# Splitting fp32 weights for TensorE: from ScalarE and VectorE to two GpSimd DMAs and a ScalarE negation

## Chip, cores and metric

The kernel runs on one core of a Trainium2 chip. The metric is device time in microseconds (us) of one execution; lower is better. Engines are called PE (TensorE, matmul; PEld its weight loads), DVE (VectorE), ACT (ScalarE), POOL (GpSimd) and SP (SyncE, which issues the DMAs of the kernel before).

## The reference

Two transformer blocks run one after the other on 512 tokens of width 1024, all in fp32:

```python
# block 1
mod = silu(c) @ w_mod + b_mod                       # six vectors: shifts, scales, gates
h = rmsnorm(x, g_pre_mix) * (1 + sc1) + sh1         # the same for 256 context tokens
u, q, k, v = split(h @ w_in)
mix = concat([pool_mixer(u), neighbourhood_attention(q, k, v, k_ctx, v_ctx, rpb)]) @ w_out
x = x + gt1 * rmsnorm(mix)
y = square(relu(modulate(x) @ w_mlp_in)) @ w_mlp_out         # 1024 -> 4096 -> 1024
x = x + gt2 * rmsnorm(y)
# block 2
parts = rmsnorm(x) @ w_in_2                         # latent attention, a gated recurrence, memory attention
x = x + concat([rmsnorm(mla), hgrn, rmsnorm(mem)]) @ w_out_2
x = x + (silu(h2 @ w_gate) * (h2 @ w_up)) @ w_down           # 1024 -> 2816 -> 1024
```

## The kernel before

A product in fp32 precision is made of three fast matmuls. Each fp32 number is split into a half `hi`, rounded to the type fp32r, and a rest `lo = raw - hi`, also fp32r. Then `w x` is summed as `w_hi x_hi + w_hi x_lo + w_lo x_hi`, which is what `mm3` does with 512 tokens as the moving operand. Activations are split where they arise. Weights arrive from HBM as 128x1024 fp32 tiles (512 KB, eight 128x128 blocks), and each is split by `weights` (L590):

- `load_raw` (L584) has SP load the tile into one of 4 slots of the class `raw`.
- `copy` makes `hi`: a cast, on ACT or POOL.
- `tt` makes `lo`: a subtraction of `hi` from the raw tile, on DVE or POOL.
- `hi` and `lo` go into slots of the class `w`, of which there are 10, so five weights are held split at a time.

With one such weight PE does 8 blocks x 3 = 24 matmuls of 128x512 (`dense_tile`, `moving_k`); `chunked` asks for the weights of one output tile. Some weights are narrower: in the last stage a 128x1024 tile of `w_down` alternates with one of 128x256.

The order of the program is not written out by hand. Every instruction is recorded by `Plan.record` with its reads and writes, and `Plan.schedule` picks, with a table of costs (`Cost`, `Machine`), the order in which each engine gets them. That order is then fixed: every engine, and SP, takes its own instructions strictly in that sequence and waits at each for the semaphores that it needs. Slots are handed out in the plan, too, so a load waits until the last reader of its slot's former tile is done.

The stages, by time in the profile: the norm of x with the modulation vectors and `w_in_v` (to 68 us); projections, neighbourhood attention, pool mixer, `w_out`, memory keys and the first `w_mlp_in` tiles (to 291 us); the first feed-forward, `w_mlp_in` and `w_mlp_out` (to 651 us); a norm (to 672 us); `w_in_2`, `w_hi` and the start of the recurrence (to 780 us); recurrence, latent and memory attention, `w_out_2` (to 965 us); the second feed-forward, `w_gate`, `w_up`, `w_down` (to the end). The two feed-forward stretches are called dense below, the others mixed.

Everything that the plan issues is called in `Plan.issue`, so the profile gives nearly all instructions one line, L508; tiles are told apart by the names of their classes (`t`, `w`, `raw`, `bank`, `tmp`, `fixed`, `big`) or of the DRAM tensor. `bank` is a PSUM bank.

Of the kernel before, what the change touches and what calls it, by code (L numbers as in the profile page):

```python
# [9 lines left out]
F = mybir.dt.float32  # L10
R = mybir.dt.float32r
I32 = mybir.dt.int32
U8 = mybir.dt.uint8
AF = mybir.ActivationFunctionType
ALU = mybir.AluOpType
# [52 lines left out]
class Tag:  # L68
    def __init__(self, cls, shape, dtype, cap=None):
        self.cls, self.shape, self.dtype, self.cap = cls, shape, dtype, cap  # L70
        self.needs = [] if cls == "fixed" else [cls] + ([cap[0]] if cap else [])
        self.users = 0
        self.writer = [None, None]
        self.readers = [[], []]
        self.slot = None
        self.real = None
        self.owner = None


class View:  # L80
# [7 lines left out]
    def rows(self, i):  # L88
        v = self[64 * i:64 * i + 64]
        v.parts = (i,)  # L90
        return v

    def rearrange(self, pattern, **kw):
# [82 lines left out]
def inputs(args, kw):  # L176
    rest = list(args[0 if "out" in kw else 1:]) + [z for k, z in kw.items() if k not in ("out", "accum_out")]
    return [z for z in rest if isinstance(z, View)]


class Cost:
# [3 lines left out]
    def __init__(self, eng, fn, args, kw):  # L185
        self.eng, self.extra, self.tail, self.port = eng, 0, TAIL[eng], False
        self.strips, self.used = (0, 1, 2, 3), 0
        if eng == "PE":
            self.extra = 160
            self.pe(fn, args, kw)  # L190
        elif eng == "SP":
            self.time = 470
        else:
            self.other(fn, args, kw)

# [42 lines left out]
class Machine:  # L238
# [38 lines left out]
    def commit(self, c, op, t):  # L277
        if c.eng == "PE":
            fin = self.pe_end(t, c.time)
            for i in c.strips:  # L280
                self.strip[i] = fin
            self.issue, self.width = t + 14, len(c.strips)
            i = int(fin // TICK)
            self.ticks[i] = self.ticks.get(i, 0) + c.used
            return fin + c.extra
        fin = self.end(c, op, t)
        self.free[c.eng] = fin - c.tail
        if c.eng == "SP":
            self.dma = max(self.dma, t + 1150) + op.nbytes / 360.0
            return self.dma + 950  # L290
        if self.load(op):
            self.table = op.table[0]
        if c.port:
            self.port[c.eng], self.turn = fin, t
        return fin + c.extra
# [13 lines left out]
class Plan:  # L309
# [13 lines left out]
    def record(self, choices):  # L323
        op = Op()
        op.idx = len(self.ops)
        op.prio = op.idx + self.shift
        op.choices = []
        for eng, fn, args, kw in choices:
            op.choices.append((eng, fn, args, kw, Cost(eng, fn, args, kw)))
        eng, fn, args, kw = choices[0]  # L330
        out = kw.get("out", args[0] if args else None)
        outs = [z for z in (out, kw.get("accum_out")) if isinstance(z, View)]
        ins = [z for z in inputs(args, kw) if not any(z is o for o in outs)]
        op.writes = {id(z.tag): z.tag for z in outs}
        op.reads = {id(z.tag): z.tag for z in ins}
        op.nbytes = 4 * math.prod(out.shape) if eng == "SP" else 0
        op.table = None
        if fn == "activation":
            op.table = TABLES.get(kw.get("func", args[2] if len(args) > 2 else None))
        deps = set(self.fence)  # L340
        for z in ins:
            deps.update(w for w in (z.tag.writer[q] for q in z.parts) if w is not None)
        raw = set(deps)
        for z in inputs(args, kw):
            raw.update(z.tag.writer[q] for q in z.parts)
        for z in outs:
            for q in z.parts:
                if z.tag.writer[q] is not None:
                    deps.add(z.tag.writer[q])
                deps.update(z.tag.readers[q])  # L350
        for z in outs:
            for q in z.parts:
                z.tag.writer[q], z.tag.readers[q] = op.idx, []
        for z in ins:
            for q in z.parts:
                if z.tag.writer[q] != op.idx:
                    z.tag.readers[q].append(op.idx)
        op.allocs = []
        for t in list(op.writes.values()) + list(op.reads.values()):
            if t.owner is None:  # L360
                t.owner = op.idx
                op.allocs.append(t)
        for t in {**op.reads, **op.writes}.values():
            t.users += 1
        deps.discard(op.idx)
        op.need = len(deps)
        op.succ = []
        op.ready = [0.0] * len(op.choices)
        for d in deps:
            self.ops[d].succ.append((op.idx, d in raw))  # L370
        self.ops.append(op)
        return op
# [108 lines left out]
    def place(self, tag):  # L481
        if tag.real is None:
# [6 lines left out]
            else:  # L489
                tag.real = self.slots.tile([128, WIDTH[tag.cls]], tag.dtype, tag=f"{tag.cls}{tag.slot}", name=n)  # L490
                if tag.shape[1] != WIDTH[tag.cls]:
                    tag.real = tag.real[:, :tag.shape[1]]
# [24 lines left out]
U_AFTER = ((2,), (1,), (0,), ())  # L517
CTX_LOAD, CTX_NORM = 0, 3
CTX_AT = {4: (0, 1), 5: (2, 3), 6: (4, 5), 7: (6, 7)}
WIDTH = {"t": 528, "raw": 1024, "w": 1024, "big": 1664, "tmp": 16}  # L520
CAPS = {'t': 54, 'raw': 4, 'w': 10, 'big': 2, 'tmp': 32, 'bank': 8}


def later(name):
    def wrap(method):
        def call(self, *args, **kw):
            keep = self.plan.shift
            self.plan.shift = keep + LATER[name]
            try:
                return method(self, *args, **kw)  # L530
            finally:
                self.plan.shift = keep
        return call
    return wrap


class Builder:
    def __init__(self, tc, a):
        self.tc, self.a = tc, a
        self.nc = self.plan = Plan(CAPS)  # L540

# [46 lines left out]

    @later("weights")
    def weights(self, src, n, raw=None, engines=None):  # L590
        if raw is None:
            raw = self.load_raw(src, n)
        hi = self.plan.tile("w", [128, 1024], R)
        lo = self.plan.tile("w", [128, 1024], R)
        self.copy(hi[:, :n], raw[:, :n], engines or ("ACT", "POOL"))
        self.tt(ALU.subtract, lo[:, :n], raw[:, :n], hi[:, :n].bitcast(F), engines)
        return hi, lo
# [113 lines left out]
    def halves(self, x, n_tok):  # L711
        hi, lo = self.pair(n_tok)
        self.split(x[:, :n_tok], hi, lo)
        return hi, lo
# [1049 lines left out]
```

## Time and profile before

| | |
|---|---|
| median of 3 runs | 1384.15 us (1383.81 to 1390.59) |
| the profiled execution | 1385.12 us, its span 1383.3 us |
| PE busy | 1338.9 us, 97% of the span |
| DVE, ACT, POOL busy | 846.7 us (61%), 571.9 us (41%), 38.6 us (3%) |
| DMA | 148.47 MB, mean 107 GB/s |
| mean granted PE clock | 0.99 of full speed |

The span is the time between the first and the last instruction of the profiled execution; 1.8 us lie around it. Matmuls overlap, and the end of each is modelled, so a busy PE need not be a PE at its peak rate: how many matmuls a stretch of time holds says more. The time that an engine stood idle is put down to what ended the wait. The chain is followed back from the last instruction to whatever released it, step by step.

### The profile page before, as it was taken

How to read it: one execution, taken by the hardware profiler on the slowest of the kernel's cores; microseconds unless marked ns; L12 is line 12 of the kernel's file. 1: busy time of each engine (PE TensorE's matmuls, PEld its weight loads, DVE VectorE, ACT ScalarE, POOL GpSimd, SP SyncE). 2: the span in 40 equal slices, each digit the busy share in tenths (PEclk: the TensorE clock that was granted, in tenths of full speed). 3: DMA queues.
4: the chain of work that ended last, by engine and by line, in shares of the span. 5: the costliest groups of instructions: out<-in, count | busy, mean ns of one | idle time of the engine just before them, and what ended most of it. 6: DMA issues, size and time to landing. Idle time of an engine off the chain costs nothing.

```text
span 1383.3 us, 18475 instructions
## 1 busy us (share of the span) xinstructions
PE 1338.9 (97%) x7202; PEld 1068.7 (77%) x7202; DVE 846.7 (61%) x1544; ACT 571.9 (41%) x952; POOL 38.6 (3%) x58
## 2 busy tenths in 40 slices
PE   6999999999999999999899899999999999999999
PEld 4777777867887888887688677778788888888887
DVE  5787889784453743445845879998864443344432
ACT  4444466544242332334435656667433222232220
POOL 1021120000000000000000000000000000000000
PEclk9999999999999999999899999999999999999999
DMA  9654654232542233323233020211322223332231
GB/s 343 216 138 140 207 186 136 93 105 87 183 151 76 82 102 99 100 92 92 91 91 107 17 66 25 76 46 47 122 76 101 97 69 91 115 107 91 69 101 59
DMA packets 48663, 148.47 MB, mean 107 GB/s; under 512 B 5568, under 2 KB 7232, under 8 KB 48576
## 3 DMA queue, kind: packets, MB, share of 16 engines
q1 hardware_dynamic: 48576, 147.30, 33.4%
q8 instruction: 56, 0.92, 0.3%
q14 instruction: 31, 0.25, 0.1%
HBM read 143.61 MB, written 2.10 MB: 105 GB/s over the span
## 4 chain that ended last, share of the span: by engine, by line
PE 88%; DVE 8%; DMA 2%; issue 1%; ACT 1%; SPq 0%; DVEq 0%; ACTq 0%
PE bank L508 88%; DVE t L508 5%; ACT t L508 1%; DVE tmp L508 1%; DMA raw<-w_mod_b 1%; DVE fixed L508 1%; DVE bank L508 1%; DMA t<-w_mod_a 0%; SPq L508 0%; DMA raw<-w_in_qk 0%; DVE w L508 0%; DVE big L508 0%; ACT w L508 0%; ACT tmp L508 0%; DVEq L508 0%
## 5 line engine op out<-in xcount | busy, mean ns | idle before, releaser
L508 PE MATMUL bank<-t,w 128*128 128x512 f32 (+1 forms) x4716 | 1098.6, 391 | 9.3 <-DVE w L508 4.0
L508 PEld LDWEIGHTS bank<-t,w 128*128 128x128 f32 x4716 | 867.8, 189 | 212.5 <-DVE t L508 6.7
L508 DVE TENSOR_TENSOR w<-raw,w 128x1024 fp32r<-128x1024 f32 (+2 forms) x217 | 250.3, 1158 | 391.4 <-PE bank L508 250.2
L508 ACT CAST w<-raw 128x1024 fp32r<-128x1024 f32 (+2 forms) x214 | 212.0, 994 | 420.2 <-PE bank L508 383.2
L508 DVE TENSOR_TENSOR t<-t,t 128x512 f32<-128x512 f32 (+4 forms) x286 | 167.9, 610 | 35.0 <-ACT t L508 28.0
L508 ACT ACTIVATE t<-t 128x256 f32<-128x256 f32 (+2 forms) x192 | 100.9, 543 | 47.7 <-DVE t L508 32.9
L508 PE MATMUL bank<-t,t 128*64 128x128 f32 (+5 forms) x796 | 92.8, 281 | 6.9 <-DVE t L508 4.3
L508 PEld LDWEIGHTS bank<-t,t 128*128 128x128 f32 (+2 forms) x796 | 73.9, 161 | 23.6 <-DVE t L508 7.7
L508 PE MATMUL bank<-w,t 128*128 128x512 f32 x312 | 76.1, 396 | 0.0
L508 ACT COPY t<-bank 128x512 f32<-128x512 f32 (+3 forms) x93 | 47.9, 518 | 67.7 <-PE bank L508 64.4
L508 ACT ACTIVATE t<-bank 128x512 f32<-128x512 f32 (+2 forms) x74 | 43.4, 587 | 72.6 <-PE bank L508 71.6
L508 PEld LDWEIGHTS bank<-w,t 128*128 128x128 f32 x312 | 57.8, 188 | 15.1 <-ACT t L508 1.3
L508 ACT CAST t<-t 128x512 fp32r<-128x512 f32 (+2 forms) x77 | 44.2, 584 | 55.1 <-DVE t L508 53.5
L508 DVE TENSOR_TENSOR t<-bank,t 128x512 f32<-128x512 f32 (+3 forms) x86 | 56.8, 661 | 8.6 <-PE bank L508 5.4
L508 PE MATMUL bank<-t,fixed 128*32 128x256 f32 (+3 forms) x246 | 38.5, 498 | 13.3 <-DMA t<-w_mod_a 12.3
L508 DVE SCALAR_TENSOR_TENSOR t<-raw,fixed,t 128x512 f32<-128x512 f32 x56 | 43.0, 810 | 12.3 <-DMA raw<-w_mod_b 12.2
L508 PE MATMUL bank<-fixed,t 128*128 128x128 f32 (+2 forms) x292 | 46.8, 279 | 3.4 <-ACT t L508 1.5
L508 PEld LDWEIGHTS bank<-fixed,t 128*128 128x128 f32 x292 | 35.3, 161 | 15.1 <-issue 5.2
L508 DVE TENSOR_TENSOR t<-t 128x512 f32<-128x512 f32 (+1 forms) x68 | 37.9, 557 | 4.5 <-DMA t<-xP 4.1
L508 DVE SCALAR_TENSOR_TENSOR t<-t,fixed,t 128x512 f32<-128x512 f32 (+3 forms) x60 | 38.4, 676 | 1.2 <-ACT t L508 0.9
L508 ACT ACTIVATE t<-bank,fixed 128x512 f32<-128x512 f32 (+2 forms) x32 | 21.8, 682 | 33.2 <-PE bank L508 33.0
L508 PEld LDWEIGHTS bank<-t,fixed 128*32 128x32 f32 (+1 forms) x246 | 13.6, 131 | 27.2 <-ACT fixed L508 12.3
(93 smaller groups left out, 552.8 us busy)
## 6 DMA issues: line engine op xcount, KB each, us to landing
raw<-w_mod_b SPq DMA_DIRECT2D x32, 512.0 KB, 3.9
raw<-w_mlp_in SPq DMA_DIRECT2D x32, 512.0 KB, 3.6
raw<-w_mlp_out SPq DMA_DIRECT2D x32, 512.0 KB, 3.8
raw<-w_in SPq DMA_DIRECT2D x22, 512.0 KB, 3.6
raw<-w_gate SPq DMA_DIRECT2D x22, 512.0 KB, 3.2
raw<-w_up SPq DMA_DIRECT2D x22, 512.0 KB, 3.2
t<-w_mod_a SPq DMA_DIRECT2D x32, 256.0 KB, 6.0
raw<-w_out SPq DMA_DIRECT2D x16, 512.0 KB, 3.8
```

The source lines that it names most:

```text
L508: getattr(engines[eng], fn)(*[real(z) for z in args], **{k: real(z) for k, z in kw.items()})
```

## The change

For every weight that isn't already loaded, `weights` now takes one slot of 128x2048, half of it `hi`, half `lo`, and issues two DMAs from POOL's queue with an ACT instruction between them:

1. a DMA from HBM into `hi` whose destination type is fp32r, so that the transfer does the cast;
2. `lo = -hi` on ACT (an activation with scale -1);
3. a DMA from HBM of the same weight onto `lo` that adds: `lo = -hi + raw`.

The raw tile in SBUF, the cast and the subtraction go. The four `w_in_v` tiles (five loads) keep the old way, since they come with a `raw`. The class `w` has 5 slots of 128x2048 instead of 10 of 128x1024, the same five weights; the 4 `raw` slots stay, now for `w_in_v`, `w_mod_b`, `rpb_b` and `pool_w`. The planner gets costs for a DMA on POOL, and since it plans anew, the whole order changes in places.

```diff
@@ View
+    def halves(self):
+        n = self.shape[1] // 2
+        v = [self[:, n * i:n * i + n] for i in range(2)]
+        for i in range(2):
+            v[i].parts = (i,)
+        return v
@@ Cost
         elif eng == "SP":
             self.time = 470
+        elif fn == "dma_start":
+            self.time, self.tail = 1000, 0
@@ Machine.commit
-        if c.eng == "SP":
-            self.dma = max(self.dma, t + 1150) + op.nbytes / 360.0
+        if op.nbytes:
+            self.dma = max(self.dma, t + (1150 if c.eng == "SP" else 1600)) + op.nbytes / 360.0
             return self.dma + 950
@@ Plan.record
-        op.nbytes = 4 * math.prod(out.shape) if eng == "SP" else 0
+        op.nbytes = 4 * math.prod(out.shape) * (2 if "accum_op" in kw else 1) if fn == "dma_start" else 0
@@
-WIDTH = {"t": 528, "raw": 1024, "w": 1024, "big": 1664, "tmp": 16}
-CAPS = {'t': 54, 'raw': 4, 'w': 10, 'big': 2, 'tmp': 32, 'bank': 8}
+WIDTH = {"t": 528, "raw": 1024, "w": 2048, "big": 1664, "tmp": 16}
+CAPS = {'t': 54, 'raw': 4, 'w': 5, 'big': 2, 'tmp': 32, 'bank': 8}
@@ Builder.weights
+        pair = self.plan.tile("w", [128, 2048], R)
+        hi, lo = pair.halves()
         if raw is None:
-            raw = self.load_raw(src, n)
-        hi = self.plan.tile("w", [128, 1024], R)
-        lo = self.plan.tile("w", [128, 1024], R)
+            self.nc.gpsimd.dma_start(hi[:, :n], src)
+            self.nc.scalar.activation(lo[:, :n], hi[:, :n].bitcast(F), AF.Copy, scale=-1.0)
+            self.nc.gpsimd.dma_start(lo[:, :n], src, accum_op=ALU.add)
+            return hi, lo
         self.copy(hi[:, :n], raw[:, :n], engines or ("ACT", "POOL"))
         self.tt(ALU.subtract, lo[:, :n], raw[:, :n], hi[:, :n].bitcast(F), engines)
         return hi, lo
```

Three places show how instructions move. In the names, the part after the last underscore only numbers the tile; on POOL the first DMA with a name is the cast into `hi`, the second the addition onto `lo`.

The start on POOL, before: after the memsets come the splits of the first two `w_in_v` loads.

```order
L508 MEMSET fixed_2_68 128x256
L508 MEMSET tmp_3_70 128x1
L508 MEMSET t_5_74 128x8
...
L508 TENSOR_SCALAR w_47_179<-raw_28_127 128x512
L508 TENSOR_TENSOR w_49_184<-raw_28_127,w_47_179 128x512
```

The same place, changed:

```order
L517 MEMSET fixed_2_68 128x256
L517 MEMSET tmp_3_70 128x1
L517 DMA w_5_74<-w_in_u 128x1024
L517 MEMSET t_8_80 128x8
...
L517 DMA w_5_74<-w_in_u 128x1024
...
L517 TENSOR_SCALAR w_51_189<-raw_27_124 128x512
L517 TENSOR_TENSOR w_51_189<-raw_27_124,w_51_189 128x512
```

Both DMAs of the first `w_in_u` weight now stand ahead of the `w_in_v` splits; before, SP loaded that tile behind all of `w_mod_a`, `masks` and `pool_w`.

POOL in the second feed-forward, changed (before, POOL has nothing there, SP one load and DVE one subtraction for each weight):

```order
L517 DMA w_2014_9487<-w_up 128x1024
L517 DMA w_2017_9514<-w_gate 128x1024
L517 DMA w_2014_9487<-w_up 128x1024
L517 DMA w_2017_9514<-w_gate 128x1024
L517 DMA w_2022_9555<-w_up 128x1024
L517 DMA w_2025_9582<-w_gate 128x1024
L517 DMA w_2022_9555<-w_up 128x1024
L517 DMA w_2025_9582<-w_gate 128x1024
```

Weights go in twos: two casts, then the two additions. With one queue in order, the third cast is behind the second addition.

The last stage, `w_down`, on DVE, before:

```order
L508 TENSOR_TENSOR w_2612_11605<-raw_2594_11490,w_2606_11564 128x1024
L508 TENSOR_TENSOR w_2616_11618<-raw_2599_11524,w_2610_11577 128x256
L508 TENSOR_TENSOR t_2619_11625<-fixed_125_409,bank_2607_11570 128x512
L508 TENSOR_TENSOR w_2620_11651<-raw_2605_11561,w_2614_11610 128x1024
L508 TENSOR_TENSOR w_2624_11664<-raw_2609_11574,w_2618_11623 128x256
L508 TENSOR_TENSOR t_2627_11671<-fixed_251_936,bank_2615_11616 128x512
```

and what carries the weights there now, on POOL:

```order
L517 DMA w_2196_11224<-w_down 128x256
L517 DMA w_2195_11194<-w_down 128x1024
L517 DMA w_2200_11240<-w_down 128x1024
L517 DMA w_2196_11224<-w_down 128x256
L517 DMA w_2201_11268<-w_down 128x256
L517 DMA w_2203_11280<-w_down 128x1024
L517 DMA w_2200_11240<-w_down 128x1024
L517 DMA w_2201_11268<-w_down 128x256
```

On DVE only the additions of the residual are left. On POOL the rows read: cast of w_2196, addition of w_2195, cast of w_2200, addition of w_2196, casts of w_2201 and w_2203, additions of w_2200 and w_2201: between the cast of a weight and its addition, which waits for ACT's negation, stand one or two DMAs of others.

## Rows read from the trace of the kernel before

**Rows 1.** The page: busy time of the engines, and the chain that ended last by engine.
```profile
PE 1338.9 (97%) x7202; PEld 1068.7 (77%) x7202; DVE 846.7 (61%) x1544; ACT 571.9 (41%) x952; POOL 38.6 (3%) x58
PE 88%; DVE 8%; DMA 2%; issue 1%; ACT 1%; SPq 0%; DVEq 0%; ACTq 0%
```
**Rows 2.** Stretches: from:to, length, busy us (xinstructions) by engine, PE clock, DMA share, GB/s.
```profile
0.00:68.00 68.00, 54.48 (x333) 40.97 (x334) 42.73 (x89) 30.69 (x58) 6.63 (x18) 1.00 0.80 282
68.00:291.00 223.00, 213.24 (x1289) 167.41 (x1287) 188.98 (x433) 117.26 (x225) 25.51 (x33) 1.00 0.45 140
291.00:651.00 360.00, 359.44 (x1577) 290.37 (x1577) 174.70 (x231) 123.25 (x163) 0.00 (x0) 1.00 0.36 112
651.00:672.00 21.00, 14.95 (x60) 10.22 (x58) 21.00 (x33) 11.87 (x19) 0.00 (x0) 0.93 0.03 10
672.00:780.00 108.00, 104.19 (x792) 83.72 (x794) 68.01 (x132) 53.15 (x90) 0.53 (x1) 0.94 0.31 93
780.00:965.00 185.00, 177.69 (x1357) 139.18 (x1346) 162.34 (x392) 117.64 (x252) 5.93 (x6) 0.97 0.17 52
965.00:1380.00 415.00, 414.80 (x1820) 336.83 (x1819) 188.52 (x238) 118.01 (x149) 0.00 (x0) 1.00 0.28 91
```
**Rows 3.** Waits of PE: what released it, us in total, times, longest.
```profile
PE bank L508 <- DMA t<-w_mod_a: 12.3, 1, 12.3
PE bank L508 <- DVE t L508: 9.6, 15, 1.6
PE bank L508 <- ACT t L508: 5.2, 10, 1.3
PE bank L508 <- DVE w L508: 4.0, 1, 4.0
```
**Rows 4.** The stretches of rows 2, instructions on `w` tiles alone (DVE third, ACT fourth).
```profile
0.00:68.00 68.00, 35.84 (x149) 27.38 (x150) 8.56 (x7) 7.22 (x7) 3.77 (x4) 1.00 0.80 282
68.00:291.00 223.00, 150.72 (x687) 114.40 (x685) 26.48 (x21) 26.14 (x25) 0.00 (x0) 1.00 0.45 140
291.00:651.00 360.00, 355.53 (x1539) 286.85 (x1539) 83.10 (x68) 68.88 (x66) 0.00 (x0) 1.00 0.36 112
651.00:672.00 21.00, 14.95 (x60) 10.22 (x58) 1.23 (x1) 2.08 (x2) 0.00 (x0) 0.93 0.03 10
672.00:780.00 108.00, 91.84 (x378) 72.97 (x378) 21.95 (x18) 18.26 (x18) 0.00 (x0) 0.94 0.31 93
780.00:965.00 185.00, 108.41 (x405) 77.27 (x405) 19.98 (x20) 14.98 (x18) 5.41 (x5) 0.97 0.17 52
965.00:1380.00 415.00, 414.46 (x1816) 336.39 (x1815) 88.99 (x82) 74.44 (x79) 0.00 (x0) 1.00 0.28 91
```
**Rows 5.** The chain that ended last, in order of time: start us, us, what.
```profile
5.49 6.67 DMA t<-w_mod_a
...
670.68 1.15 DVE w L508
```
**Rows 6.** DMA issues: count, KB each, median us from issue to landing.
```profile
raw<-w_mlp_in SPq DMA_DIRECT2D x32, 512.0 KB, 3.6
...
raw<-w_in_v SPq DMA_DIRECT2D x3, 512.0 KB, 6.0
...
raw<-w_down SPq DMA_DIRECT2D x8, 128.0 KB, 2.7
```
**Rows 7.** Instructions on `w` and `raw` tiles: ns min/median/max, first and last start, forms.
```profile
L508 DVE TENSOR_TENSOR w<-raw,w x217: 419/1225/1997, 25.7 to 1365.7; 128x1024 fp32r<-128x1024 f32 x88, 128x512 fp32r<-128x512 f32 x12, 128x256 fp32r<-128x256 f32 x8, 128x768 fp32r<-128x768 f32 x1
L508 ACT CAST w<-raw x214: 407/1050/1063, 24.6 to 1359.1; 128x1024 fp32r<-128x1024 f32 x102, 128x512 fp32r<-128x512 f32 x3, 128x768 fp32r<-128x768 f32 x2
L508 POOL TENSOR_TENSOR w<-raw,w x3: 1262/1272/1692, 16.3 to 898.3; 128x512 fp32r<-128x512 f32 x3
L508 DVE SCALAR_TENSOR_TENSOR t<-raw,fixed,t x56: 739/747/1559, 73.6 to 381.0; 128x512 f32<-128x512 f32 x56
L508 SPq DMA_DIRECT2D raw<-w_mod_b x32: 327/328/524, 62.2 to 374.5; - x32
```

## The prediction, made before the change was run

> **What bounds the kernel now.** I read the page first: PE is busy 97% of the span, and 88% of the chain that ended last is PE, 8% DVE [rows 1]. The table of stretches then separates two kinds of time [rows 2]. In the dense stretches, 291 to 651 and 965 to 1380 us, PE is idle for 0.6 and 0.2 us and starts 1577 and 1820 matmuls, one each 228 ns in both. Weights come early enough there, so a faster way to split them gains nothing; it can only lose. In the other stretches PE is idle for 68 - 54.5 = 13.5, then 9.8, 6.1, 3.8 and 7.3 us. Of the first, 12.3 us are one wait for the first `w_mod_a` tiles [rows 3], which no split shortens. That leaves 28.2 us, and it is all that a relief of DVE can give directly. The clock adds a little: it is granted at 0.93, 0.94 and 0.97 of full speed between 651 and 965 us [rows 2], the stretches in which PE also stood idle; that is 0.07 x 21 + 0.06 x 108 + 0.03 x 185 = 13.5 us of lost clock, part of which returns if the waits do.
>
> The waits of PE say what ends this idle time [rows 3]: DVE's work on activations 9.6 us in 15 short waits, ACT's 5.2 us, and one wait of 4.0 us for the subtraction of a weight. The chain shows that one: at 670.7 us it runs through a DVE instruction on `w`, just behind the norm in which DVE was busy for all 21 us [rows 5, 2].
>
> **What is removed.** 217 subtractions on DVE and 3 on POOL, all but the five of `w_in_v` [rows 7]. In the dense stretches that takes 83 and 89 us off DVE [rows 4] at no gain. In the mixed ones it takes 8.6 + 26.5 + 1.2 + 22.0 + 20.0 = 78 us [rows 4] from 43 + 189 + 21 + 68 + 162 = 483 us that DVE is busy there [rows 2], 16%. Of the 28.2 us, the wait for a subtraction goes whole: 4.0 us. For the other 24.2 the bounds are 16% of the 9.6 us that PE waits for DVE's activations, 1.5 us, and all of it. I take 6.5, near the lower end, since the DVE instructions that PE waits for depend on each other and keep their durations; what goes is a subtraction queued between them. **Gain 10.5 us, bounds 5.5 and 28.2.** Late next there: the same DVE work on activations.
>
> ACT's cast becomes a negation of the same 128x1024 elements, 1.05 us by the cast's row [rows 7]; I cost the difference at nothing. SP's loads of weights go, one issue of 0.33 us each [rows 7], off the path.
>
> **What is added on the DMA engines.** One transfer of 512 KB becomes two, one of which also reads its destination. At 112 GB/s the 16 engines are busy 36% of the time, at 91 GB/s 28% [rows 2], so full use is 311 to 325 GB/s and 512 KB take 1.6 to 1.7 us of all engines. No cast and no addition is in this trace. The bounds for both together are two plain transfers, 3.3 us, and four, if each costs double, 6.6 us. I take three, 5.0 us, because only the addition has a second source. PE uses a weight in 24 x 228 ns = 5.5 us, so 5.0 us stays hidden behind it, with the engines some 90% busy. The Trainium skill ("Collectives: The Full Stack", The bandwidth ceiling) says that an adding transfer reads two sources and so runs at half the rate of a copy, the add itself being free. By that, addition and cast are 3.3 + 1.65 us, what I take; no run so far shows it.
>
> **What is added on POOL.** 215 weights, two DMAs each. The nearest rows for the time that one holds POOL are 0.33 us for an SP issue and 1.27 us for a POOL instruction on half a tile [rows 7]. A landing takes 3.6 us where the DMA engines are little used, 6.0 us where they are 80% busy [rows 6, 2]. In the dense stretches the queue runs cast, cast, addition, addition. The second addition waits for the second cast's landing and ACT's 1.05 us, and the next cast is behind it. So two weights hold the queue for a landing, a negation and two issues: 3.6 + 1.05 + 0.7 = 5.3 us at least, 6.0 + 1.05 + 2.5 = 9.6 us at most. PE needs two in 10.9 us. Hidden at both ends; the cover is the five slots, and if a landing rose to 7.4 us it would be gone.
>
> The last stage has less cover. There a tile of 1024 columns alternates with one of 256, 24 + 6 matmuls, so two weights are wanted every 6.8 us. The same sum gives 5.3 to 9.6 us: a loss of 0 to 2.8 us for each of the eight pairs (the narrow tiles number 8 [rows 6]), 0 to 22 us. I take a landing of 4.5 us, nearer to the 3.6 us of this kind of load, and an issue in the middle, 0.8: 7.15 us, **2.5 us in all**.
>
> **What is moved.** The first `w_in_u` weight is now cast at the very start, beside the loads on SP whose last, at 5.5 us, gates PE until 12.2 us [rows 5]. In the first stretch 282 GB/s keep the engines 80% busy [rows 2]: full use is 353 GB/s, and 512 KB more cost 1.5 us, the cast and the addition at three transfers 4.5 us; nothing, if they fill gaps. I take **2.0 us**, since SP no longer loads that tile later in the stretch. ACT's negation of it waits for the landing, and behind it on ACT are the first splits of x, which wait for the same loads. POOL's additions stand ahead of the pool mixer's and the memsets; these had long waits before them and only hold POOL.
>
> **The sum.** The profiled execution took 1385.1 us: a span of 1383.3 and 1.8 around it. 1385.1 - 10.5 + 2.5 + 2.0 = 1379.1 us. The median of the three runs is 1.0 us lower than that execution, so I forecast **1378 us**, and on the same scale the own range of this case is 1370 to 1385 us.
>
> **Rivals.**
> *The DMA engines become the bound (slower).* If the cast, too, costs two transfers, a weight takes 6.6 us of all engines where PE uses it in 5.5. The point that decides is 5.5 us. The price is 1.1 us for each of the 68 + 82 = 150 weights of the dense stretches [rows 4], 170 us: about 1550 us. For it: the engines change the type of each word and nothing here shows at what rate. Against it: only one of the two reads two sources.
>
> *The chain cast, negation, addition is late (slower).* Landings of 6.0 us, which 90% busy engines may well give, cost the last stage 22 us instead of 2.5. In the mixed stretches ACT holds its queue 2.4 us longer at each of some 62 negations, 149 us of 331 us busy there [rows 2]; ACT is 1% of the chain [rows 1], 14 us, 4% of that work, so about 6 us reach the end. 1378 + 20 + 6 = 1404 us.
>
> *DVE and POOL hold each other off (slower).* Single DVE instructions took 1997 instead of 1225 ns and 1559 instead of 747 [rows 7]: some 0.8 us in which another engine's instruction had to end. If each of the 124 DMAs that POOL issues for those 62 weights did this to DVE or was held by it, that is 99 us; DVE is on the chain for 8% of 1383, 111 us, 23% of its work there, so 23 us arrive: 1401 us. Against it: most DVE instructions show their median. The Trainium skill ("SBUF — State Buffer", SBUF: two separate sides) warns of just this: a DMA issued from GpSimd has its descriptors written there, and a DVE copy in a two-port mode locks it out, so it advises the ACT or SP queue. What the trace shows fits a lock of some kind; it shows no such DMA.
>
> *The whole idle time goes (faster).* If DVE's queue was the cause of all short waits, 28.2 us and most of the 13.5 us of clock return: 1385 - 41 + 2 = 1346 us at best. Against it: ACT and the matmuls' own order end part of the waits [rows 3].
>
> **How the numbers follow.** About 0.5%, 6.9 us, is what a measurement can tell from no change. I give the forecast 0.44, nearly half of it below 1377.2 us; the large gain, below 1370 us, 0.18; the late chain and the lock together 0.22, between 1386 and 1440 us, 0.05 of it within the bound; the DMA bound 0.16. Faster: 0.21 + 0.18 = 0.39. Same: 0.23 + 0.05 = 0.28. Slower: 0.17 + 0.16 = 0.33. The range of 1355 to 1450 us leaves out nearly all of the DMA bound and the far end of the large gain, some 2 in 10. Both signs hold much of it, so I repeat the likeliest case's own range, 1370 to 1385.
>
> **What would show it.** Right: DVE some 250 us less busy, one matmul each 228 ns in both dense stretches, no wait of PE for a `w` tile, landings near 4 us. The DMA bound would show as PE waiting for additions all through 291 to 651 us with the DMA share near 1; the late chain as such waits in the last 55 us alone and as ACT waiting for casts; the lock as DMA issues far over 1.3 us on POOL or DVE instructions far over their medians. A wait of PE in a dense stretch makes the forecast wrong.

## The result, and the profile after

The changed kernel takes **1404.45 us** (median of 4 runs, 1399.54 to 1406.1) against 1384.76 us (1383.81 to 1390.59): a ratio of 1.0127, interval [1.009, 1.0165]. Slower, outside the likeliest case's own range and within the wide one. Its profiled execution took 1404.54 us.

The page after: busy time, the DMA queue of POOL, the chain by engine.

```profile
PE 1343.8 (96%) x7202; PEld 1074.4 (77%) x7202; DVE 620.4 (44%) x1339; ACT 571.2 (41%) x951; POOL 337.0 (24%) x479
...
q0 software_dynamic: 61920, 210.00, 66.3%
...
PE 76%; DVE 8%; DMA 4%; issue 4%; ACT 2%; POOL 1%; DVEq 0%; POOLq 0%; ACTq 0%
```

DVE lost 226 us of work [rows 1], yet PE's share of the chain fell from 88 to 76%: DMA and issue have come onto it. The stretches, moved along with the program's own stages (columns as in [rows 2]):

```profile
0.00:70.00 70.00, 54.64 (x306) 39.08 (x307) 39.47 (x83) 26.92 (x50) 11.78 (x25) 1.00 0.92 308
70.00:300.00 230.00, 217.07 (x1317) 173.17 (x1317) 159.79 (x409) 120.97 (x230) 55.56 (x76) 0.99 0.75 194
300.00:660.00 360.00, 357.72 (x1554) 288.45 (x1553) 101.13 (x166) 122.29 (x160) 91.35 (x128) 1.00 0.83 193
...
980.00:1400.00 420.00, 414.66 (x1816) 336.17 (x1814) 108.70 (x161) 116.40 (x149) 115.24 (x161) 1.00 0.80 184
```

The dense stretches hold nearly as many matmuls as before (1554 for 1577 and 1816 for 1820), with the DMA engines at 0.83 and 0.80 instead of 0.36 and 0.28 [rows 2]. Where the time is lost shows best when one follows the weight matmuls: there are 5028 with a weight tile in every kernel, and the table gives how much later than before some of them start (us, counted from 0, worked out from the instructions' start times in one profiled execution of each kernel; the rows below `after` are the experiments of the next section). The 450th ends the front (projections and the first attention heads), the 2250th the first feed-forward, the 3450th lies just behind the start of the second, the 4800th just ahead of its last stage.

```
kernel                        450th   2250th   3450th   4800th     last
before (starts at)            176.7    620.7   1021.5   1334.0   1379.8
after                         +15.3    +13.0    +15.2    +15.0    +19.1
ctl_all_old                    -0.6     -2.6     +2.8     +2.8     +2.9
e1_front_old                   -0.1     -3.3     -4.5     -4.9     -1.0
e4_front_new                  +10.9     +8.8    +15.0    +15.1    +15.3
e6_add64                       +8.0     +5.8     +0.9     +0.8     +0.8
e12_neg_pool                   +9.8     +7.9    +11.2    +11.0    +14.6
e21_mod_no_wait                +7.4     +4.0    +10.9    +10.7    +14.8
e22_before_no_wait             -2.3     -2.5     -4.8     -4.8     -4.8
e19_price_front                +1.8     +0.2     +7.9     +7.6    +11.7
e10_price                      +4.4     +5.3     -2.3     -1.8     +3.1
e16_price6000                  +2.9     +8.8    +18.0    +17.9    +21.5
e13_price_add64                +0.1     +3.0     -3.1     -3.6     -3.5
e14_price_front_old            -0.5     +1.3     +1.0     +2.1     +7.3
e17_price_both_old             -0.2     +1.0     -0.1     +0.8     +0.8
e3_both_old                    -1.3     -3.8     -7.2    +38.7    +38.9
e20_price_mid_new              -1.9     -1.4     -1.7     -1.6     -1.6
```

So the 19 us are +15 in the front, +4 in the last stage, and about nothing between. In the front, the stretches of the kernel before and of the one after, at the same places in the program:

```profile
24.00:68.00 44.00, 43.95 (x273) 34.41 (x266) 32.00 (x66) 20.87 (x37) 1.19 (x4) 1.00 0.74 260
68.00:115.00 47.00, 45.25 (x284) 37.24 (x283) 36.83 (x86) 20.63 (x41) 11.29 (x13) 1.00 0.56 160
115.00:177.00 62.00, 59.71 (x391) 46.15 (x390) 50.88 (x139) 31.66 (x63) 5.83 (x8) 1.00 0.53 166
```

```profile
27.00:75.00 48.00, 45.28 (x264) 34.29 (x265) 30.94 (x69) 16.80 (x29) 5.52 (x10) 1.00 0.90 293
75.00:127.00 52.00, 48.55 (x287) 39.10 (x287) 33.98 (x86) 23.88 (x45) 17.09 (x21) 0.97 0.88 226
127.00:192.00 65.00, 60.02 (x387) 47.48 (x386) 40.38 (x124) 33.88 (x65) 13.45 (x20) 0.97 0.59 154
```

The DMA engines are nearly full there until 127 us, where before they had a quarter to a half of their time free. Of the 15 us some 3.5 are clock (an estimate: 0.03 of 52 and of 65 us). It was granted at 0.50 of full speed, the lower of its two levels, from 76 to 79 and from 141 to 144 us, each time just behind waits of PE (1.3 and 0.5 us, then 4.4 us). What waits for the DMA engines, after, in the first 192 us (us in total, times, longest), and one of these waits on ACT:

```profile
DVE t L517 <- DMA raw<-w_mod_b: 22.7, 7, 6.4
...
ACT w L517 <- DMA w<-w_in_qk: 13.3, 5, 6.9
ACT w L517 <- DMA w<-w_in_u: 7.1, 1, 7.1
```

```profile
72.32 1.06 ACT L517 ACTIVATE w<-w 128x1024 fp32r<-128x1024 f32 x1 [7.14 <-DMA w<-w_in_u]
```

Before, DVE waited 4.5 us for `w_mod_b` up to 177 us, and ACT 12.5 us for the loads of `w_in_qk` and `w_in_u` that it cast. The `w_mod_b` loads are not weights of matmuls: DVE multiplies them into the modulation vectors that are wanted much later. But DVE takes its instructions in the plan's order, so a late load holds back the attention's work behind it. ACT is held in the same way, here 7.1 us by a negation whose cast had not landed. Both are on the chain that ended last (start us, us, what):

```profile
83.38 9.09 DMA w<-w_in_qk
92.49 1.06 ACT w L517
...
116.31 9.13 DMA raw<-w_mod_b
...
132.08 5.82 DMA raw<-w_mod_b
...
140.18 10.33 PE bank L517 x63
```

PE's own waits hardly name a weight at all:

```profile
PE bank L517 <- DMA t<-w_mod_a: 12.9, 2, 12.7
PE bank L517 <- DVE t L517: 11.4, 11, 4.4
PE bank L517 <- ACT t L517: 9.5, 13, 1.4
...
PE bank L517 <- DMA w<-w_down: 3.3, 3, 1.6
```

The last of them is the last stage, seen in the chain there (start us, us, what):

```profile
1354.13 8.41 DMA w<-w_down
...
1380.14 4.06 DMA w<-w_down
1384.30 1.07 ACT w L517
1385.66 6.34 DMA w<-w_down
```

Issues and landings (count, KB, median us to landing; then ns min/median/max that one DMA holds POOL, where a cast is near the minimum and an addition near the median):

```profile
w<-w_mlp_in POOLq DMA_DIRECT2D x64, 512.0 KB, 6.1
...
raw<-w_mod_b SPq DMA_DIRECT2D x32, 512.0 KB, 5.6
...
w<-w_down POOLq DMA_DIRECT2D x32, 512.0 KB, 5.5
w<-w_in_qk POOLq DMA_DIRECT2D x16, 512.0 KB, 6.5
```

```profile
L517 POOL DMA_DIRECT2D w<-w_mlp_in x64: 542/865/892, 266.2 to 596.1; - x64
```

### The profile page after: what moved, and what is told of

It reads as the page before. It is cut to its first block, busy times and chain, and to the rows that moved or that the text cites. A ratio compares the mean times of both kernels' runs of the same rounds, so it can differ in the third digit from the quotient of the medians.

```text
span 1402.8 us, 18605 instructions
## 1 busy us (share of the span) xinstructions
PE 1343.8 (96%) x7202; PEld 1074.4 (77%) x7202; DVE 620.4 (44%) x1339; ACT 571.2 (41%) x951; POOL 337.0 (24%) x479
## 4 chain that ended last, share of the span: by engine, by line
PE 76%; DVE 8%; DMA 4%; issue 4%; ACT 2%; POOL 1%; DVEq 0%; POOLq 0%; ACTq 0%
PE bank L517 76%; DVE t L517 6%; DMA w<-w_down 1%; ACT t L517 1%; DMA raw<-w_mod_b 1%; POOL w L517 1%; DVE tmp L517 1%; DMA w<-w_in_qk 1%; DMA w<-w_in 1%; DMA w<-w_mem_v 1%; DVE big L517 1%; DVE bank L517 0%; DMA w<-w_out 0%; ACT w L517 0%; DVE fixed L517 0%
## 5 line engine op out<-in xcount | busy, mean ns | idle before, releaser
L517 ACT ACTIVATE w<-w 128x1024 fp32r<-128x1024 f32 (+3 forms) x215 | 214.7, 1000 | 471.9 <-DMA w<-w_up 116.2
L517 DVE TENSOR_TENSOR t<-t,t 128x512 fp32r<-128x512 f32 (+3 forms) x290 | 168.3, 604 | 103.2 <-ACT t L517 93.5
L517 ACT ACTIVATE t<-t 128x512 f32<-128x512 f32 (+2 forms) x191 | 100.2, 542 | 73.9 <-DVE t L517 63.4
L517 POOL DMA_DIRECT2D w<-w_mlp_out x64 | 46.1, 769 | 141.4 <-ACT w L517 70.8
L517 POOL DMA_DIRECT2D w<-w_mlp_in x64 | 47.0, 783 | 122.3 <-ACT w L517 72.2
L517 PEld LDWEIGHTS bank<-w,t 128*128 128x128 f32 x312 | 61.0, 197 | 16.2 <-issue 2.0
L517 POOL DMA_DIRECT2D w<-w_out x48 | 34.4, 740 | 159.9 <-PE bank L517 106.3
L517 POOL DMA_DIRECT2D w<-w_down x64 | 45.7, 777 | 99.9 <-ACT w L517 50.4
L517 ACT CAST t<-t 128x512 fp32r<-128x512 f32 (+1 forms) x76 | 43.2, 579 | 32.7 <-DVE t L517 32.0
L517 POOL DMA_DIRECT2D w<-w_in x44 | 32.1, 762 | 101.2 <-ACT w L517 55.3
L517 POOL DMA_DIRECT2D w<-w_up x44 | 36.5, 836 | 82.1 <-ACT w L517 63.8
```

The source lines that it names most:

```text
L517: getattr(engines[eng], fn)(*[real(z) for z in args], **{k: real(z) for k, z in kw.items()})
```

## The experiments

The first four expectations weigh three theories: **A**, the added transfers fill the DMA engines in the front; **B**, the new order and slots cost the time by themselves; **C**, the chain of cast, negation and addition holds the queues of ACT and POOL. Weights "the old way" are loaded by SP, cast and subtracted, into the new pair slots. The kernel before is measured anew beside each group of runs; ratios are to that.

### Which part of the change: three mixtures

```diff
-        if raw is None:
+        if raw is None and by_load(name, k0):
+            raw = self.load_raw(src, n)
+        if raw is None:
             self.nc.gpsimd.dma_start(hi[:, :n], src)
```

`by_load` holds for `w_in_u` and `w_in_qk` (e1), for all (ctl), for all but these two (e4).

> The weights of the first attention block (w_in_u, w_in_qk, 12 tiles) come by SP load, cast and subtraction as before; all others by the two DMAs. Theory A (the DMA engines, used 90% up to 127 us, are what the front waits for): the 450th weight matmul starts near 178 us instead of 192, and 13 to 15 us return: about 1390 us. Theory B (the loss is spread, made by the new order and slots as such): 1400 us or more, the 450th at 185 us or later.

> No weight comes by the two DMAs, but the slots are those of the change (5 of 2048 columns, hi and lo freed together) and the planner plans anew. Theory A: 1385 us, within 4 of before. Theory B (double slots or another order cost by themselves): 1395 us or more.

> Only the 12 tiles of the first attention block come by the two DMAs, all others as before. Theory A: the front alone carries the loss: 1397 to 1400 us, the 450th weight matmul near 192 us. Theory B: 1385 to 1390 us.

Measured: e1 1384.01 us, 0.9992 [0.9981, 1.0002]; ctl 1387.82, 1.0011 [1.0, 1.0022]; e4 1401.69, 1.0118 [1.0093, 1.0143]. The twelve weights of the front by two DMAs are enough for most of the front's loss, and without them it is gone. B falls as a cause by itself: new slots and a new plan cost 0.1%. In the table e4 loses 10.9 us by the 450th matmul and nothing in the last stage, e1 nothing in the front and 4.0 in the last stage. That e4's total comes so near to 1404 is in part chance: it loses 6.2 us between the 2250th and the 3450th matmul, where ctl loses 5.4 as well and the change 2.2.

### The additions' bytes

```diff
+            if "accum_op" in kw:
+                args = [z[:, :64] for z in args]
             getattr(engines[eng], fn)(*args, **...)
```

> The changed kernel in its order and with its waits, but each addition covers only the first 64 columns, so the other columns of lo stay -hi: the additions' traffic is left out, nothing else. Theory A (traffic): the front returns 8 to 13 us, total 1391 to 1396 us, DMA share in the front under 0.8. Theory B (order): 1402 to 1406 us, since the order is the same. Theory C (the chain of cast, negation and addition in the queues): half way, 1398 to 1401 us, since only the additions' landings get shorter.

Measured: 1380.34 us, 0.9966 [0.9952, 0.9979], below what each theory gave; its profiled execution was its slowest, 1386.25. With order, slots, casts and all waits kept, taking the additions' bytes out gains 24 us. It shortens the additions' own landings, too (3.1 us for `w_in_qk`), so it does not tell full engines from a shorter chain. The front's casts land no earlier for it: 6.9 us for `w_in_qk`, 6.5 in the change for its casts and additions together. Of the last stage's 4.1 us nothing is left (+0.8 to +0.8). In the front half of the loss stays in the profiled execution, +8.0. Some 3.3 us of that are clock (an estimate): from 94 to 101 us it was granted at 0.53 while PE was busy for 6.0 us. The mean granted clock of this execution was 0.985, that of the nine others 0.991 to 0.995, so less of the front's loss may be left in them; no trace shows it.

### What a transfer costs by itself

A kernel that only moves tiles of 512 KB: loads from SP, loads, casts and additions from POOL, alone and eight in a row.

```diff
+nc.sync.dma_start(z.bitcast(F), s)          # load
+nc.gpsimd.dma_start(z.bitcast(F), s)        # load from POOL
+nc.gpsimd.dma_start(z, s)                   # cast
+nc.gpsimd.dma_start(z, s, accum_op=ALU.add) # addition
```

> Transfers of 512 KB alone: loads from SP, the same loads from POOL, casts and additions from POOL, each singly twice and eight at a time twice; it computes nothing of the reference. As the prediction took it: eight plain loads land within 8 x 1.65 = 13 us and some 2 us, casts the same, additions in twice that, 26 us. If a cast costs double, 26 us as well; if the addition costs as little as a load, 15 us. A single landing of 4.0 us or less for a cast would put the 6.5 us seen in the front down to full DMA engines; 6 us or more down to the kind of DMA.

The chain in time; the time that one issue holds POOL (busy us, mean ns); and the start of the eight additions, of which the first seven are one group and the last stands in the chain above:

```profile
0.74 3.33 DMA spload<-w_mlp_in
...
8.89 3.58 DMA cast<-w_mlp_in
...
15.51 5.48 DMA add<-w_mlp_in
...
68.39 3.63 POOL cast L1797 x7
72.01 9.90 DMA cast<-w_mlp_in
...
91.16 16.08 DMA add<-w_mlp_in
```

```profile
L1811 POOL DMA_DIRECT2D add<-w_mlp_in x18 | 15.5, 863 | 35.6 <-ACT add L1806 22.9
L1794 POOL DMA_DIRECT2D poolload<-w_mlp_in x18 | 9.7, 561 | 64.0 <-DMA outT<-zero 32.1
L1797 POOL DMA_DIRECT2D cast<-w_mlp_in x18 | 9.5, 564 | 28.0 <-DVE tok L1788 28.0
```

```profile
84.32 6.52 POOL L1811 DMA_DIRECT2D add<-w_mlp_in  x7 [11.70 <-ACT add L1806]
```

All this is one execution. Eight casts take 72.01 + 9.90 - 68.39 = 13.5 us, eight additions 91.16 + 16.08 - 84.32 = 22.9. From the second tile on that is (13.5 - 3.6) / 7 = 1.4 us for a cast and (22.9 - 5.5) / 7 = 2.5 us for an addition, 3.9 for a weight. A cast is no dearer than a load, the addition costs 1.7 times as much. A lone weight needs 3.6 + 1.1 + 5.5 = 10.2 us from the cast's issue to the addition's landing. Alone, a cast lands in 3.6 us, so the 6.5 us of the front are not the kind of DMA; what is left is how full the engines are there.

### ACT's queue in the front

```diff
+            if eng == "ACT" and kw.get("scale") == -1.0 and op.choices[ci][2][0].tag in self.on_pool:
+                nc.gpsimd.tensor_scalar(args[0], args[1], -1.0, 0.0, ALU.mult, ALU.add)
+                continue
```

> The changed kernel's order, slots and DMAs, but the 12 negations of the front (w_in_u, w_in_qk) run on POOL at their place in the order instead of on ACT, so that ACT's queue is not held while a cast lands. If the half of the front's loss that stays when the additions are cut to 64 columns is ACT held by negations that wait (13 us of such waits up to 190 us), the 450th weight matmul starts some 5 to 8 us earlier than 192.1 us and the whole takes 1397 to 1400 us. If full DMA engines alone make the loss, 1404 to 1406, with the 450th matmul at 191 to 194 us.

Measured: 1408.65 us, 1.0156 [1.0139, 1.0173]. The runs do not agree among themselves: the profiled execution took 1400.09 us and has the 450th matmul at +9.8, the other four took 1405 to 1410. Inconclusive for the front. It does not decide C either: the negations now wait in POOL's queue instead, 29.8 us for these casts in the first 192 us (15.5 and 14.3), and the casts and additions behind them wait along.

### DVE's queue in the front

```diff
+            if eng == "DVE" and fn == "scalar_tensor_tensor" and kw["in0"].tag in self.mod:
+                kw["in0"] = kw["in1"]
```

and likewise for the first product of each sum, which reads a broadcast column. `mod` holds the `raw` tiles of `w_mod_b`.

> The changed kernel's order, slots and transfers, but DVE's products with w_mod_b read another tile that is there already (the second to fourth modulation vectors are then computed from other data), so that DVE's queue no longer waits for those loads, 22.7 us up to 190 us. The loads stay; they are held back by nothing but their queue and run somewhat earlier. If DVE held by late loads is the larger part of the front's loss, the 450th weight matmul starts 8 to 15 us before 192.1 us and the whole takes 1388 to 1397 us. If the loss lies in transfers that PE or ACT wait for directly, the 450th stays at 188 to 192 us and the whole at 1400 to 1405.

> The control: the same replacement in the kernel before, whose DVE waits 5.0 us for those loads up to 190 us. If its waits cost nothing there, 1383 to 1387 us and the 450th weight matmul at 175 to 178 us; what it gains beyond that has to be taken off the gain of the changed kernel.

Measured: 1397.04 us, 1.0068 [1.0045, 1.0091], and for the control 1381.91, 0.997 [0.9959, 0.998]. The 450th matmul comes at +7.4 instead of +15.3, in the control at -2.3: 7.9 - 2.3 = 5.6 us, over a third of the front's loss, are DVE held by late `w_mod_b` loads, and what PE's clock lost by it: e21 has the clock at 1.00 through the front. The place fits: between the 300th and the 350th weight matmul the changed kernel loses 6.0 us, behind the two `w_mod_b` waits of the chain above, and e21 0.8. It is less than expected, and it rests on one execution of each kernel. ACT still waits as long for its casts (16.2 + 6.6 us up to 190 us, after 20.4), and what DVE now waits for is ACT:

```profile
DVE t L523 <- ACT t L523: 34.5, 17, 5.4
```

### The planner's price of a landing

```diff
-            self.time, self.tail = 1000, 0
+            self.time, self.tail = 700, 0
-            self.dma = max(self.dma, t + (1150 if c.eng == "SP" else 1600)) + op.nbytes / 360.0
+            self.dma = max(self.dma, t + (1150 if c.eng == "SP" else 4000)) + op.nbytes / 360.0
```

e16 has 6000 in place of 4000; e19 has the 4000 for the DMAs of `w_in_u` and `w_in_qk` alone, and the 1000; e13 is e10 with the additions cut to 64 columns.

> The change as it is, with the planner's two figures for a DMA on POOL set near what the profile shows: 700 instead of 1000 ns of the engine, 4000 instead of 1600 ns before its bytes move. The order is planned anew. If the front's loss comes of negations placed too early in ACT's queue, because the planner takes a landing for shorter than the 6.5 us that it takes there, the loss shrinks by 5 to 10 us: 1394 to 1399 us. If the traffic makes it, the order helps little: 1401 to 1406 us.

> The change, with 4000 ns as the planner's price before the bytes move for the 24 DMAs of w_in_u and w_in_qk alone, 1600 as in the change for all others. If the planner's short price of the landing there makes the front's loss, the 450th weight matmul starts at 179 to 184 us, as with 4000 everywhere, and not at 192. The rest of the plan may come out otherwise; the whole 1385 to 1398 us. If the price elsewhere matters, 188 to 193 us.

> The change, with 700 and 6000 ns as the planner's figures for a DMA on POOL. If the loss goes with the price of the landing, because a longer one makes the planner issue casts and additions earlier, this stays at or below the 1388 us of 4000 ns: 1384 to 1390. If 1388 was one lucky order among many, this falls anywhere between 1384 and 1408 us.

> The kernel whose plan takes a POOL DMA's landing as 4000 instead of 1600 ns before its bytes move, with the additions cut to 64 columns, so that most of their traffic is gone (lo of the other columns stays minus hi). With the plan of the change itself that cut was worth 24 us. If it is worth that much whatever the plan, this gives 1364 us. If the plan has taken over that loss already, since weights are now issued early enough for full DMA engines, only the last stage's 4 to 5 us and a part of the front's 5 us come back: 1378 to 1384 us.

Measured: e10 1388.1 us, 1.001 [1.0, 1.002]; e19 1398.32, 1.0087 [1.0061, 1.0113]; e16 1406.56, 1.0151 [1.0134, 1.0168]; e13 1381.53, 0.9974 [0.9964, 0.9983]. The front answers to the price alone, whatever comes later: +15.3 us at 1600, +4.4 at 4000, +2.9 at 6000, +1.8 with 4000 in the front only. The traffic is the same: e10's stretches there have the DMA engines as full as after.

```profile
27.00:75.00 48.00, 47.91 (x286) 36.37 (x285) 33.04 (x72) 21.34 (x37) 5.82 (x11) 1.00 0.90 289
75.00:127.00 52.00, 51.51 (x313) 42.14 (x312) 35.64 (x92) 22.85 (x44) 17.22 (x22) 1.00 0.85 231
```

The landings are as late, too: up to 190 us `w_mod_b` takes 5.8 us in e10 and `w_in_qk` 7.1, where it is 5.5 and 6.5 after. What goes is the waiting in the queues: ACT for the front's casts 20.4 us after, 5.6 in e10 (these two rows), and DVE for `w_mod_b` 22.7 after, 14.0 in e10 and 2.0 in e16 (third row, e16 apart).

```profile
DVE t L517 <- DMA raw<-w_mod_b: 14.0, 8, 5.4
...
ACT w L517 <- DMA w<-w_in_u: 2.9, 1, 2.9
ACT w L517 <- DMA w<-w_in_qk: 2.7, 2, 2.3
```

```profile
DVE t L517 <- DMA raw<-w_mod_b: 2.0, 1, 2.0
```

e13 then shows the additions' bytes under the better plan: 1388.1 to 1381.5, 6.6 us instead of 24, with the front at +0.1 and the last stage at 0. e16 stays slow for another reason: it loses 5.9 us between the 450th and the 2250th matmul and 9.2 between the 2250th and the 3450th. So 1388 for the whole was in part a lucky order; the front's answer was not.

### Is there a version that beats both

e3 and e17 leave `w_in_u`, `w_in_qk` and the `w_down` weights of the last stage (rows 12 to 21, 16 tiles) the old way, with the planner's own figures and with 700 and 4000; e14 leaves the front alone with the latter; e20 uses two DMAs for block 2's attention weights only.

```diff
+    return name in ("w_in_u", "w_in_qk") or name == "w_down" and k0 >= 12
```

> The 12 weights of w_in_u and w_in_qk and the last 10 w_down weights (rows 12 to 21) are split the old way, all others by two DMAs; the plan is made anew. If the loss is made by the two DMAs of the front and of the end alone, and the gain of some 4 us that the run with the front alone showed against the kernel before up to 700 us is real, this gives 1379 to 1382 us, faster than both. If the tail's loss is not the two DMAs but the new slots, it gives 1384 like the run with the front alone. If the plan's chance order decides, it may fall anywhere up to 1388.

> The same plan figures, the front and the last 10 w_down weights the old way, all others by two DMAs. With the planner's own figures this choice cost 38 us, because from 1250 us on only one weight was under way at a time: cast 3.4, negation 1.1 and addition 5.4 us stood in a row against 5.5 us of matmuls. If that is because the planner takes landings for short, it is gone here: 1376 to 1381 us, faster than the kernel before. If it is because w_down's tiles take the slots early, it stays: 1410 us or more.

> The same plan figures (700 and 4000 ns), w_in_u and w_in_qk split the old way, all other weights by two DMAs. If the front's remaining loss of some 5 us (450th weight matmul at 181.1 instead of 176.7 us) is the two DMAs' traffic there, it goes and the gain of some 9 us between 640 and 985 us stays: 1380 to 1384 us. If the plan's chance order decides, anything from 1380 to 1395 us.

> Two DMAs for the weights of latent and memory attention and the recurrence in block 2 alone (w_mem_v, w_in_2, w_hi, w_uq, w_uk, w_uv, w_out_2), all others the old way, the planner's figures 700 and 4000. Front, dense stretches and last stage as in the kernel before. If the relief of DVE there is worth 9 us, as one plan showed it between 640 and 985 us, 1375 to 1380 us, faster than both. If that was one plan's order, 1383 to 1391 us.

Measured: e3 1425.61 us, 1.0276 [1.0261, 1.0292]; e17 1386.32, 1.0002 [0.9992, 1.0013]; e14 1391.76, 1.0045 [1.003, 1.0061]; e20 1387.13, 1.0007 [0.9997, 1.0016]. None beats the kernel before: e3 and e17 miss their ranges, e14 and e20 fall where chance order was to put them. The miss of e3 shows what stands behind the cover of five slots. Its chain towards the end of the second feed-forward, and a stretch of it:

```profile
1267.18 3.49 DMA w<-w_gate
...
1270.78 1.07 ACT w L517
...
1272.13 5.33 DMA w<-w_gate
...
1283.15 3.40 DMA w<-w_up
...
1286.71 1.07 ACT w L517
...
1288.06 5.42 DMA w<-w_up
```

```profile
1300.00:1330.00 30.00, 12.02 (x37) 7.68 (x35) 2.77 (x4) 3.36 (x4) 2.82 (x4) 0.69 0.32 70
```

One weight at a time: cast, negation, addition, 10.3 us in a row for 5.5 us of matmuls, and a granted clock of 0.69 of full speed where PE stood idle for more than half of the time. The cost was 45.9 us between the 3450th and the 4800th matmul. With the other prices (e17) it is 0.9. Whether the `w_down` tiles took the slots early was not tried by itself.

## Why the prediction was wrong

**The step that failed is "What is moved": the front was priced at 2.0 us and cost 15.** The 2.0 us stood for one weight at the very start, and that is about what came: the first weight matmul starts at 26.8 us instead of 24.2. The working counted the bytes of this weight against a resource that was 80% busy and stopped there. Three things were missing. Not one but twelve weights fall into the first 192 us, each with 3.9 us of transfers instead of 1.4 (e8). On engines that are full, other transfers become late: `w_mod_b` landed in 5.5 us up to 190 us instead of 3.8. And the late ones stand in fixed queues, DVE's and ACT's, ahead of work that PE needs. The runs show each link: without the additions' bytes the front loses 8.0 us, part of it clock, or with the better plan 0.1 (e6, e13); without DVE's wait 5.6 less (e21, e22); with casts and loads priced as long as they take, 1.8 to 4.4 (e10, e19). I had read the planner's new costs in the diff and not held them against the 6.0 us of [rows 6]: it takes 1.6 + 1.5 + 0.95 us for a cast's landing, 4.0 us, where 6.5 came. A plan fixed on short landings puts the waiting instructions too early. What ACT's waits alone cost of the 15 us stays open, since e12 was inconclusive. In the sum, 1379.1 us against 1404.5, this step makes 13.3 us of the miss, the next one 10.5 and the last stage 1.6.

**The gain of 10.5 us did not come.** DVE's relief was as large as said (226 us less busy), but between the 2250th and the 3450th matmul, where block 2's mixed stretches lie, nine plans with two DMAs there (after, e1, e3, e10, e14, e16, e17, e19, e20) stand at -7.7 to +9.2 us, on average +0.6, and the three with the old split (before, ctl, e4) at 0, +5.4 and +6.2. The means are some 3 us apart, and the scatter is larger: after, e12 and e21, which share one plan for this stretch, have +2.2, +3.3 and +6.9. So no gain is shown; e20, which does that part alone, has 1.0007. The lower bound, 5.5 us, was already too high. [rows 3] are waits for DVE's chain of activations; that the subtraction in between only filled time in which this chain waited for others would explain it, but was not tried. (The 78 us said to go also held the three `w_in_v` subtractions on DVE, 3.7 us, which stay: 15%, not 16.)

**Right: the dense stretches.** DVE is 226 us less busy where some 250 were said, and landings are 6 us and not near 4, but there is no PE wait for `w_mlp_in`, `w_mlp_out`, `w_gate` or `w_up`: from the 3450th to the 4800th matmul 312.5 us before, 312.3 after. Three transfers' worth for a weight was near enough: 5.0 us taken, 3.9 in a row in e8, some 4.6 here (an estimate: 0.83 of 360 us for 64 weights and 4 loads of `w_mod_b`), the rival's 6.6 excluded. The Trainium skill ("Collectives: The Full Stack", The bandwidth ceiling) gives the adding transfers of a collective half the rate of a copy; e8 shows 13.5 / 22.9 = 0.59 of the cast's.

**Right in kind, near in size by luck: the last stage.** 2.5 us taken, 4.1 measured, 3.6 to 5.2 in all eight kernels that move all of `w_down` by two full DMAs, and at most 0.2 in all the others. Landings of `w_down` took 5.5 us for the wide tiles and 4.6 to 5.0 for the narrow ones, not 4.5, and an issue 0.55 or 0.86 us, not 0.8. With these the same sum gives 5.5 + 1.07 + 0.55 + 0.86 = 8.0 us a pair, 1.2 too much for each of the eight, some 9 us: twice what came. So the sum overstates what a queue that is held costs PE here; why is not shown.

**The rivals.** The late chain gave 1404 us, the number that came, but by 22 us in the last stage and 6 from ACT in all mixed stretches; the chip shows 4 there, and 15 in the front, where ACT held by late casts, as this rival had it, is a part, and DVE held by other loads, which it did not name, another. A right total by a wrong place proves nothing, and the table by stages tells the two apart. The lock of DVE and POOL is not seen: DVE's products on `raw` have a median of 746 ns after and 747 before [rows 7], and `w_mlp_in`'s 64 DMAs held POOL for at most 892 ns, `w_down`'s for at most 1209. The Trainium skill ("SBUF — State Buffer", SBUF: two separate sides) warns of that lock; no run here shows it at a price. The idle time did not go: PE's waits for DVE's and ACT's activations rose from 9.6 + 5.2 [rows 3] to 11.4 + 9.5 us.

## What to carry to other kernels

Before a change adds transfers, look at the DMA share stage by stage, and for a stage that is already near full ask which other transfers become late and which engine's queue they stand in, not only whether the new ones are in time. Where a planner fixes the order, hold its price of every new operation against a measured landing: 1.6 instead of 4.0 us cost 11 to 13.5 us in the front alone. And an engine's busy time is no measure of a relief: 226 us less DVE work brought no gain that stands out of the scatter between plans.

## What the runs showed of the hardware

- A DMA of 512 KB from POOL that changes f32 to fp32r runs about as fast as a plain load (eight in 13.5 us, singly 3.6 us; a load singly 3.6 from POOL and 3.3 from SP, e8). One that adds takes 5.5 us singly and 22.9 for eight.
- An issue holds POOL 0.56 us for a load or a cast, 0.86 us for an addition (e8), against 0.33 us on SP [rows 7].
- A load that PE never waits for can lie on the chain that ended last: in the kernel before, the chain up to 190 us runs for 12 us through loads of `w_mod_b`, from 68.5 to 88.4 us, though DVE waited only 5.0 us for them up to there. Taking these waits away all through the program, 16.1 us of DVE's time, gave 4.0 us (e22). PE's waits had shown nothing of it.
